# A decoder layer with product-key experts: 24 dense expert columns for 16, dense rows loaded ahead of the second product, and a finer-spread zero fill

## The chip, the cores and the metric

The kernel runs on one core of a Trainium2 chip. The metric is device microseconds (us) of one execution. Engines: PE is TensorE (matmuls; PEld its weight loads), DVE is VectorE, ACT is ScalarE, POOL is GpSimd and SP is SyncE, which here issues most of the DMAs. SPq rows are DMA issues of SP's queue.

## The reference, cut to what matters

One layer on 256 tokens of width 1024, all float32: a gated position mixer and an attention, their sum through `w_out`, a LayerNorm that gives `h`, the expert block below, and a last LayerNorm. The change touches the expert block alone, and the writing of zeros that prepares it:

```python
def peer_ffn(h, w_q, sub_keys, u_tab, v_tab):
    q = (xt @ w_q).reshape(n_tok, PEER_HEADS, 2, PEER_KEY_HALF)
    s = jnp.einsum('thpk,pnk->thpn', q, sub_keys)
    top_s, top_i = lax.top_k(s, PEER_TOPK)                    # 16 of 128 keys, twice
    ...                                                       # 16 of the 256 pairs: 16 of 128 x 128 experts
    gates = jax.nn.softmax(best_s, axis=-1)                   # for each of 8 heads
    hid = jax.nn.gelu(jnp.einsum('chkd,cd->chk', u_tab[ec], xc), approximate=False)
    y = jnp.einsum('chk,chkd->cd', gc * hid, v_tab[ec])
```

So each token picks 8 x 16 of 16,384 experts. An expert is a row of `u_tab` and a row of `v_tab`, both 1024 wide.

## The kernel before, in words

**Products.** Every float32 product is made of three matmuls on a split of each operand into `hi` and `lo` (fp32r). ACT writes `hi` (`do_hi`, line 125), DVE writes `lo` as the raw tile less `hi` (`do_lo`, line 135, its subtraction at line 145). Weight tiles of 128x1024 come through a ring of raw buffers: `do_load` (line 108) issues an SP load at line 121, or, for a tile whose rows stand in a list, an indirect DMA of POOL at line 117. `advance` (line 148) keeps three `hi` and two `lo` tiles ahead of PE and loads as far as raw buffers are free. The ring has 4 buffers, and from a point in U on 9 more (`RING`).

**The order.** All of the work is a list of steps, one weight tile each; the loop at line 1192 goes through it. At each step it advances the weight stream, calls the step's `before`, its matmuls, the previous step's `post` and the step's `after`, and then `run_stages`, which takes one turn of each generator in `stages`, and `run_queue`, which gives out some DVE work of the expert choice. What is written first stands first on each engine's queue.

**HG and its zeros.** `HG` is a DRAM array with a row for each expert: for both blocks of 128 tokens the hidden value and the gate. `fill_task` (line 274) writes zeros to its gates of block 0: the rows 0 and NX+1 to ROWS-1 whole (line 278, 127 rows in the second of the two), and then 32 fills of 256 KB (line 281), with three turns of the generator for each. It starts at step 16. `wo_before` (line 589), at the first step of the `w_out` product, runs all generators to their end, so all fills left are issued there.

**U.** The first expert product is dense: 128 tiles of 128 experts (`uexp_mm`, line 1042), all experts for all tokens. After every second tile ACT makes the GELU of both and SP writes them to HG (line 1056). The gates are added into HG by 128 indirect DMAs of POOL (line 752) for one block, and by a dense write for the other.

**V.** The second expert product takes `DENSE` = 16 tiles of 128 experts in a row, and 90 slot tiles whose 128 experts come from lists: two of `CAP_A` = 23 tiles of experts that tokens of one block alone use, and one of `CAP_B` = 44 for those of both blocks. The lists (`list_task`, line 973, its last line 1033) are made during U. A tile of a list costs POOL two gathers: rows of `peer_v` (line 117) and rows of HG (line 1098); a dense tile costs SP two loads (lines 121 and 1091). `wprep` (line 1101) multiplies hidden values and gates (DVE, line 1107) and splits the product into `wsp` (ACT line 167, DVE line 168); `vexp_mm` (line 1111, matmuls at line 1120) makes 12 matmuls of 512 columns for a tile of both blocks, 6 for one of one block. `slots` (line 1073) is the order: six dense tiles, then both, A, both, B and so on, with the other dense tiles put between. `vexp_before` (line 1160) loads HG rows `HG_AHEAD` = 6 tiles ahead and prepares `wsp` two ahead; at tile 0 it calls `v_open`. Experts beyond the lists' capacity would go through `overflow` (line 1127), behind a branch at line 1139.

**The end.** The last tiles' matmuls (line 1224) close the four sums, then come the residual, LayerNorm and the stores (lines 1226 to 1261).

Of the kernel before, what the change touches and what calls it, by code (L numbers as in the profile page):

```python
# [28 lines left out]
NK = 128  # L29
# [5 lines left out]

U_, V_, Q_, K_, VV_, GA_, GB_ = range(7)
NX = NK * NK
ROWS = NX + 128
ROW = 2 * T
CAP_A, CAP_B = 23, 44  # L40
SLOTS = 2 * CAP_A + CAP_B
DENSE, FIRST = 16, 6
UNITS = DENSE + SLOTS
COLG = 8
LISTG = 8
FILL = 4
HG_AHEAD = 6
RING = 9
RAW_BUFS = 4
HI_AHEAD = 3  # L50
LO_AHEAD = 2
# [8 lines left out]
def block_kernel(ctx, tc, a, out):  # L60
# [7 lines left out]
    def open_pool(name, **kw):  # L68
        kw.setdefault("bufs", 1)
        es = ExitStack()  # L70
        pool = es.enter_context(tc.tile_pool(name=name, reuse_waits="tile", **kw))
        return pool, es
# [9 lines left out]
    def acc(shape=(128, 512)):  # L82
        return ps1.tile(list(shape), F32, name="acc", tag="acc", bufs=4)
# [12 lines left out]
    ring, ring_pos, load_cap = [], [0], [None]  # L96

    def add_item(src, shape, dst=None, pieces=1):
        items.append((src, shape, dst, pieces))
        return len(items) - 1  # L100
# [65 lines left out]
    def split_to(hi, lo, src):  # L166
        nc.scalar.copy(hi, src)  # L167
        nc.vector.tensor_sub(lo, src, hi.bitcast(F32))  # L168
# [6 lines left out]
    def run_stages():  # L175
        for g in list(stages):
            try:
                next(g)
            except StopIteration:
                stages.remove(g)  # L180
# [13 lines left out]
    def drain_queue():  # L194
        while queue:
            try:
                if next(queue[0]) is None:
                    raise RuntimeError("background work waits for a later step")
            except StopIteration:
                queue.popleft()  # L200


    def mm3(ps, lh, ll, rh, rl, start, stop):
        for i, (l, r) in enumerate(((lh, rh), (lh, rl), (ll, rh))):
            nc.tensor.matmul(ps, l, r, start=start and i == 0, stop=stop and i == 2)  # L205
# [31 lines left out]
    def row_bcast(dst, src):  # L237
        n = src.shape[-1]
        nc.sync.dma_start(dst, bass.AP(tensor=src.tensor, offset=src.offset, ap=[[0, 128], [1, n]]))
# [16 lines left out]
    def step(item, mm, post=None, before=None, after=None, hi_cap=None, lo_cap=None):  # L256

        steps.append((item, mm, post, before, after, hi_cap, lo_cap))
# [11 lines left out]
    nc.vector.memset(zero, 0.0)  # L270
    HG = dram.tile([ROWS, 2, 2, 128], F32, name="HG")
    hview, *gview = dram_disjoint_views(HG[:, :, :, :], 2 + TOPK)

    def fill_task():

        for r in (slice(0, 1), slice(NX + 1, ROWS)):
            n = r.stop - r.start
            nc.sync.dma_start(HG[r, :, :, :].rearrange("r t w c -> r (t w) c"), zero[:n, None, :].to_broadcast([n, 4, 128]))
        rows = HG[1:NX + 1, :, :, :].rearrange("(p r) t w c -> p r t w c", p=128)
        for r in range(0, NK, FILL):  # L280
            nc.sync.dma_start(rows[:, r:r + FILL, 0, 1, :], zero[:, None, :].to_broadcast([128, FILL, 128]))
            yield
            yield
            yield
    eps = const.tile([128, 1], F32, name="eps")
# [604 lines left out]
    def gate_pass():  # L890
# [40 lines left out]
        def save():  # L931
# [6 lines left out]
            cell["vp"] = vp  # L938
            ring.extend([(vp, "raw2", RING)] * RING)
            ring_pos[0] = RAW_BUFS  # L940
# [101 lines left out]
    def uexp_mm(it, i):  # L1042
        wh, wl = parts.pop(it)
        if i % 2 == 0:
            hid[i // 2] = acc((128, 2, T))
        ps = hid[i // 2]
        for k in range(8):
            mm3(ps[:, i % 2, :], wh[:, k, :], wl[:, k, :], cell["hh"][:, k, :], cell["hl"][:, k, :], k == 0, k == 7)

    def uexp_post(i):  # L1050
        ps = hid.pop(i // 2)
        h = cell["keep"].tile([128, 2, T], F32, name="hid", tag="hid", bufs=2)
        nc.scalar.activation(h, ps, AF.Gelu)
        for k in range(2):
            r = (i - 1 + k) * NK + 1
            nc.sync.dma_start(hview[r:r + NK, :, 0, :], h[:, k, :].rearrange("p (t c) -> p t c", t=2))

    uit = [add_item(a["peer_uT"][i], [128, 8, 128]) for i in range(NK)]
    for i in range(NK):
        step(uit[i], lambda i=i: uexp_mm(uit[i], i), (lambda i=i: uexp_post(i)) if i % 2 else None)  # L1060

    def v_open():
        drain_queue()
        for n in range(HG_AHEAD):
            hg_load(n)
        cell["z"] = hpool.tile([128, 2, D], F32, name="z", tag="hh")
        cell["ln2"] = hpool.tile([128, 2, D], F32, name="ln2", tag="hl")
        nc.sync.dma_start(cell["z"], cell["res_d"])
        row_bcast(cell["ln2"][:, 0], a["ln2_g"])
        row_bcast(cell["ln2"][:, 1], a["ln2_b"])  # L1070
# [16 lines left out]
    def hg_load(n):  # L1087
        kind, s = slots[n]
        hg = cell["vp"].tile([128, 2, 2, 128], F32, name="hg", tag="hg", bufs=HG_AHEAD + 1)
        if kind == 3:  # L1090
            nc.sync.dma_start(hg, HG[1 + s * NK:1 + (s + 1) * NK, :, :, :])
            hgs[n] = hg
            return
        if kind == 2:
            dst, src = hg.rearrange("p t w c -> p (t w c)"), HG[:, :, :, :].rearrange("r t w c -> r (t w c)")
        else:
            dst, src = hg[:, 0].rearrange("p w c -> p (w c)"), HG[:, :, :, :].rearrange("r t w c -> (r t) (w c)")
        nc.gpsimd.indirect_dma_start(dst, None, src, bass.IndirectOffsetOnAxis(ap=cell["grow"][:, s:s + 1], axis=0))  # L1098
        hgs[n] = hg

    def wprep(n):

        m = len(TOKS[slots[n][0]])
        hg = hgs.pop(n)
        w = cell["vp"].tile([128, 2, 2, 128], F32R, name="wsp", tag="wsp", bufs=3)
        hv = hg[:, :m, 0, :]
        nc.vector.tensor_mul(hv, hv, hg[:, :m, 1, :])  # L1107
        split_to(w[:, 0, :m], w[:, 1, :m], hv)
        wsp[n] = w
# [50 lines left out]
    def vexp_before(n):  # L1160
        if n == UNITS - EARLY:
            overflow()
        if n == 8:
            cell["reg"] = nc.values_load(cell["extra"][0:1, 0:1], min_val=0, max_val=NX)
        if n == 0:
            while stages:
                run_stages()
            ps1_es.close()
            yp, cell["y_es"] = open_pool("yp", space=PSUM)
            ys = {k: yp.tile([128, 512], F32, name=f"y{k[0]}{k[1]}") for k in ((1, 0), (1, 1), (0, 0), (0, 1))}  # L1170
            cell["Y"] = [[ys[t, c] for c in range(2)] for t in range(2)]
            v_open()
            wprep(0)
            wprep(1)
        if n + HG_AHEAD < UNITS:
            hg_load(n + HG_AHEAD)
        if n + 2 < UNITS:
            wprep(n + 2)

    vit = []  # L1180
    for n, (kind, s) in enumerate(slots):
        if kind == 3:
            vit.append(add_item(a["peer_v"][s * NK:(s + 1) * NK, :].rearrange("p (a b) -> p a b", a=2), [128, 2, 512]))
        else:
            vit.append(add_item(a["peer_v"], [128, 2, 512]))
            row_lists[vit[n]] = lambda s=s: cell["vrow"][:, s:s + 1]
        step(vit[n], lambda n=n: vexp_mm(n), None, lambda n=n: vexp_before(n))
# [4 lines left out]
    for n, (item, mm, post, before, after, hi_cap, lo_cap) in enumerate(steps):  # L1192
        if pending and item == vit[0]:
            pending()
            pending = None
        advance(item, hi_cap, lo_cap)
        early_consts(n)
        if n == FILL_AT:
            stages.append(fill_task())
        if n == BIAS_AT:  # L1200
            stages.append(bias_task())
        if before:
            before()
        if n < len(steps) - EARLY:
            mm()
        if pending:
            pending()
        pending = post
        if after:
            after()  # L1210
        run_stages()
        run_queue(AUX_BUDGET)
# [121 lines left out]
```

## Time and profile before

| | us |
|---|---|
| median of 3 runs | 1081.35 (1080.59 to 1082.46) |
| the profiled execution | 1080.72 |
| its span | 1079.0 |
| U, dense product over 128 tiles, ends about | 776 |
| V begins | 785 |
| mean granted clock of TensorE, of full speed | 0.974 |

PE is busy 997.8 us of the span (92%), DVE 764.5 (71%), ACT 515.0 (48%) and POOL 449.2 (42%). These shares are averages over stages with different limits; the prediction reads single stages. A timeline row gives the start and the duration of one instruction (or of a run of like ones), and in brackets the idle time of its engine just before it and what ended that. A windows row gives a stretch and its length, the busy time and the instructions (x) of PE, PEld, DVE, ACT and POOL in it, PE's granted clock as a share of full speed, the mean busy share of the 16 DMA engines, and GB/s.

### The profile page before, as it was taken

To read this page: it belongs to the slowest core of one execution; us is meant where nothing else is said; L and a number is where in the kernel's file an instruction comes from. 1 tells how busy PE (TensorE), PEld (TensorE's weight loads), DVE (VectorE), ACT (ScalarE), POOL (GpSimd) and SP (SyncE) were. 2 spreads that over 40 slices of the span, in tenths; PEclk is the share of its full clock that TensorE was granted. 3 is DMA by queue.
4 is the path that set the end of the run, shared out by engine and by line. 5 is a ranking of instruction groups with operands and counts; after the bars stand their busy time and mean duration, and the time that the engine had idled before them with its cause. 6 is when DMAs were issued, how large, how long until landed. Compare 5 with 4: busy or idle time off the path is not lost. (4 is left out here: it accounts for less than half of the span.)

```text
span 1079.0 us, 18829 instructions
## 1 busy us (share of the span) xinstructions
PE 997.8 (92%) x7066; PEld 906.5 (84%) x7066; DVE 764.5 (71%) x1442; ACT 515.0 (48%) x747; POOL 449.2 (42%) x315
## 2 busy tenths in 40 slices
PE   9998999995999999989999999999789888998884
PEld 6988999994799999979999999999777666776663
DVE  6865655573779999997877769744367666666667
ACT  6535655542545554544355543344345444454443
POOL 0000000000000478778777873000257778787670
PEclk9999999997999999999999999999989999899998
DMA  7768556888455689887878889997888887878761
GB/s 274 273 205 281 160 181 205 275 270 252 142 215 170 165 223 217 217 208 187 185 186 193 179 227 325 306 387 227 245 285 273 281 285 258 272 263 270 247 195 44
DMA packets 151038, 249.60 MB, mean 231 GB/s; under 512 B 29360, under 2 KB 97881, under 8 KB 150553
## 3 DMA queue, kind: packets, MB, share of 16 engines
q1 hardware_dynamic: 113817, 183.47, 52.3%
q0 software_dynamic: 37120, 64.83, 23.9%
q8 instruction: 57, 0.93, 0.3%
q14 instruction: 44, 0.36, 0.1%
HBM read 212.26 MB, written 37.56 MB: 232 GB/s over the span
## 5 line engine op out<-in xcount | busy, mean ns | idle before, releaser
L145 DVE TENSOR_TENSOR lo<-raw,hi 128x1024 fp32r<-128x1024 f32 (+1 forms) x340 | 412.0, 1214 | 117.7 <-PE acc L205 63.7
L132 ACT CAST hi<-raw 128x1024 fp32r<-128x1024 f32 (+1 forms) x340 | 354.1, 1044 | 289.6 <-PE acc L205 157.4
L752 POOL DMA_INDIRECT HG<-gates,gidx x128 | 229.9, 1796 | 384.4 <-DVE ts L786 321.4
L205 PE MATMUL acc<-h_hi,hi 128*128 128x256 f32 x1152 | 327.8, 285 | 0.3 <-ACT hi L132 0.3
L205 PE MATMUL acc<-h_hi,lo 128*128 128x256 f32 x1152 | 324.9, 282 | 3.4 <-DVE lo L145 3.3
L205 PE MATMUL acc<-h_lo,hi 128*128 128x256 f32 x1152 | 322.2, 280 | 0.0
L1120 PE MATMUL y<-hi,wsp 128*128 128x512 f32 x664 | 223.7, 410 | 41.0 <-ACT wsp L167 34.7
L205 PEld LDWEIGHTS acc<-h_hi,lo 128*128 128x128 f32 x1152 | 217.1, 188 | 7.5 <-DVE lo L145 6.4
L205 PEld LDWEIGHTS acc<-h_hi,hi 128*128 128x128 f32 x1152 | 217.4, 189 | 0.6 <-ACT hi L132 0.5
L205 PEld LDWEIGHTS acc<-h_lo,hi 128*128 128x128 f32 x1152 | 217.5, 189 | 0.0
L1120 PEld LDWEIGHTS y<-hi,wsp 128*128 128x128 f32 x664 | 128.2, 193 | 87.0 <-ACT wsp L167 47.5
L117 POOL DMA_INDIRECT raw<-in_peer_v,vrow x90 | 103.2, 1147 | 146.2 <-DMA raw<-in_peer_v 95.3
L1120 PE MATMUL y<-lo,wsp 128*128 128x512 f32 x332 | 133.5, 402 | 0.0
L1098 POOL DMA_INDIRECT hg<-HG,grow x90 | 111.3, 1236 | 33.3 <-issue 23.8
L167 ACT CAST wsp<-hg 128x256 fp32r<-128x256 f32 (+1 forms) x106 | 38.1, 359 | 126.7 <-DVE hg L1107 82.4
L205 PE MATMUL acc<-xh,hi 128*128 128x256 f32 x320 | 92.9, 290 | 0.0
L205 PE MATMUL acc<-xh,lo 128*128 128x256 f32 x320 | 91.3, 285 | 0.0
L205 PE MATMUL acc<-xl,hi 128*128 128x256 f32 x320 | 91.2, 285 | 0.0
L1120 PEld LDWEIGHTS y<-lo,wsp 128*128 128x128 f32 x332 | 64.1, 193 | 13.5
L168 DVE TENSOR_TENSOR wsp<-hg,wsp 128x256 fp32r<-128x256 f32 (+1 forms) x106 | 39.0, 368 | 49.7 <-ACT wsp L167 37.8
L1107 DVE TENSOR_TENSOR hg<-hg 128x256 f32<-128x256 f32 (+1 forms) x106 | 38.5, 363 | 39.3 <-DMA hg<-HG,grow 28.9
L205 PEld LDWEIGHTS acc<-xl,hi 128*128 128x128 f32 x320 | 62.2, 194 | 0.2
(254 smaller groups left out, 1271.4 us busy)
## 6 DMA issues: line engine op xcount, KB each, us to landing
raw<-in_peer_uT SPq DMA_DIRECT2D x128, 512.0 KB
HG<-hid SPq DMA_DIRECT2D x128, 128.0 KB
HG<-zero SPq DMA_DIRECT2D x32, 256.0 KB
raw<-in_w_qk SPq DMA_DIRECT2D x16, 512.0 KB
raw<-in_w_q SPq DMA_DIRECT2D x16, 512.0 KB
HG<-G SPq DMA_DIRECT2D x16, 512.0 KB
raw<-in_peer_v SPq DMA_DIRECT2D x16, 512.0 KB
raw<-in_w_u SPq DMA_DIRECT2D x8, 512.0 KB
```

The lines of the kernel that those rows point to most:

```text
L117: nc.gpsimd.indirect_dma_start(r.rearrange("p a b -> p (a b)"), None, items[i][0], bass.IndirectOffsetOnAxis(ap=row_lists[i](), axis=0))
L132: nc.scalar.copy(parts[i][0][:, c], raws[i][:, c])
L145: nc.vector.tensor_sub(lo[:, c], r[:, c], hi[:, c].bitcast(F32))
L167: nc.scalar.copy(hi, src)
L168: nc.vector.tensor_sub(lo, src, hi.bitcast(F32))
L205: nc.tensor.matmul(ps, l, r, start=start and i == 0, stop=stop and i == 2)
L752: ins = nc.gpsimd.indirect_dma_start(gview[k].rearrange("r t w (c o) -> (r t w c) o", o=1), bass.IndirectOffsetOnAxis(ap=gidx[:, c:c + 1], ...
L1098: nc.gpsimd.indirect_dma_start(dst, None, src, bass.IndirectOffsetOnAxis(ap=cell["grow"][:, s:s + 1], axis=0))
L1107: nc.vector.tensor_mul(hv, hv, hg[:, :m, 1, :])
L1120: nc.tensor.matmul(cell["Y"][t][c], w[:, wp, j, :], v[q][:, c, :], start=(t, c) not in started, stop=n == last[t] and wp == 1)
```

## The change

There are 24 dense tiles instead of 16, and the lists shrink to 22, 22 and 40 tiles: 84 slot tiles for 90, 108 tiles in all for 106. A function `dense_start` is added, called after each U tile: at tile 120 of 128 it empties the queue of list work, runs the generators until the ring has its second part, and issues the HG loads of the first six dense tiles; at tile 127 it prepares `wsp` of tiles 0 and 1. `v_open` and `vexp_before` lose that work. HG rows are loaded 8 tiles ahead instead of 6, and the second part of the ring has 8 buffers for 9. The zero fill puts out a fill at every second step instead of every third, and ROWS is one larger, so that the fill at its end covers 128 rows.

```diff
--- before.py
+++ after.py
@@ -35,17 +35,17 @@
 
 U_, V_, Q_, K_, VV_, GA_, GB_ = range(7)
 NX = NK * NK
-ROWS = NX + 128
+ROWS = NX + 129
 ROW = 2 * T
-CAP_A, CAP_B = 23, 44
+CAP_A, CAP_B = 22, 40
 SLOTS = 2 * CAP_A + CAP_B
-DENSE, FIRST = 16, 6
+DENSE, FIRST = 24, 6
 UNITS = DENSE + SLOTS
 COLG = 8
 LISTG = 8
 FILL = 4
-HG_AHEAD = 6
-RING = 9
+HG_AHEAD = 8
+RING = 8
 RAW_BUFS = 4
 HI_AHEAD = 3
 LO_AHEAD = 2
@@ -279,7 +279,6 @@
         rows = HG[1:NX + 1, :, :, :].rearrange("(p r) t w c -> p r t w c", p=128)
         for r in range(0, NK, FILL):
             nc.sync.dma_start(rows[:, r:r + FILL, 0, 1, :], zero[:, None, :].to_broadcast([128, FILL, 128]))
-            yield
             yield
             yield
     eps = const.tile([128, 1], F32, name="eps")
@@ -1055,13 +1054,25 @@
             r = (i - 1 + k) * NK + 1
             nc.sync.dma_start(hview[r:r + NK, :, 0, :], h[:, k, :].rearrange("p (t c) -> p t c", t=2))
 
+    def dense_start(i):
+
+        if i == NK - 8:
+            drain_queue()
+            while len(ring) == RAW_BUFS:
+                run_stages()
+            for n in range(FIRST):
+                hg_load(n)
+        if i == NK - 1:
+            wprep(0)
+            wprep(1)
+
     uit = [add_item(a["peer_uT"][i], [128, 8, 128]) for i in range(NK)]
     for i in range(NK):
-        step(uit[i], lambda i=i: uexp_mm(uit[i], i), (lambda i=i: uexp_post(i)) if i % 2 else None)
+        step(uit[i], lambda i=i: uexp_mm(uit[i], i), (lambda i=i: uexp_post(i)) if i % 2 else None,
+             lambda i=i: dense_start(i))
 
     def v_open():
-        drain_queue()
-        for n in range(HG_AHEAD):
+        for n in range(FIRST, HG_AHEAD):
             hg_load(n)
         cell["z"] = hpool.tile([128, 2, D], F32, name="z", tag="hh")
         cell["ln2"] = hpool.tile([128, 2, D], F32, name="ln2", tag="hl")
@@ -1170,8 +1181,6 @@
             ys = {k: yp.tile([128, 512], F32, name=f"y{k[0]}{k[1]}") for k in ((1, 0), (1, 1), (0, 0), (0, 1))}
             cell["Y"] = [[ys[t, c] for c in range(2)] for t in range(2)]
             v_open()
-            wprep(0)
-            wprep(1)
         if n + HG_AHEAD < UNITS:
             hg_load(n + HG_AHEAD)
         if n + 2 < UNITS:
```

What this does to the order of instructions is shown at three places. First SP's queue at the start of the `w_out` product, before and then after; L281 is a zero fill.

```order
L121 DMA raw<-in_w_out 128x1024 x2
L281 DMA HG<-zero 128x4x128 x13
L239 DMA bc_l1g<-in_ln_g 128x1024
L239 DMA bc_l1b<-in_ln_b 128x1024
L239 DMA bc_pgb<-in_ple_b_gate 128x1024
L601 DMA iota<-in_iota 128x128
L602 DMA keysT<-in_keysT 128x256
L121 DMA raw<-in_w_out 128x1024
```

```order
L121 DMA raw<-in_w_out 128x1024 x2
L281 DMA HG<-zero 128x4x128 x4
L239 DMA bc_l1g<-in_ln_g 128x1024
L239 DMA bc_l1b<-in_ln_b 128x1024
L239 DMA bc_pgb<-in_ple_b_gate 128x1024
L600 DMA iota<-in_iota 128x128
L601 DMA keysT<-in_keysT 128x256
```

Thirteen fills in a row have become four; nine of them now stand earlier, among the weight loads of the products before. The next place is SP's queue at the end of U, before and after; L1056 (L1055 after) writes hidden values to HG, L1091 (L1102) loads rows of dense tiles from HG, and `raw` of `in_peer_v` are V's dense weight tiles.

```order
L121 DMA raw_9136<-in_peer_v 128x1024
L121 DMA raw_9166<-in_peer_v 128x1024
L1056 DMA HG<-hid 256x1x128 x12
L121 DMA raw_9495<-in_peer_v 128x1024
L1091 DMA hg<-HG 128x512 x6
L1068 DMA z<-res_d 128x2048
```

```order
L1055 DMA HG<-hid 256x1x128 x2
L121 DMA raw_9185<-in_peer_v 128x1024
L1102 DMA hg<-HG 128x512 x6
L1055 DMA HG<-hid 256x1x128 x6
L121 DMA raw<-in_peer_v 128x1024
L1055 DMA HG<-hid 256x1x128 x4
L1079 DMA z<-res_d 128x2048
```

The six HG loads moved from behind the last write of hidden values to ahead of the last ten writes. The third place is POOL at the same point; L752 (L751) is the last of the gate additions, L117 gathers rows of `peer_v`, L1098 (L1109) rows of HG.

```order
L752 DMA HG<-gates_3217,gidx 8454144x1 x128
L117 DMA raw_9201<-in_peer_v,vrow 128x1024
L117 DMA raw_9231<-in_peer_v,vrow 128x1024
L117 DMA raw_9266<-in_peer_v,vrow 128x1024
L117 DMA raw_9296<-in_peer_v,vrow 128x1024
L117 DMA raw_9331<-in_peer_v,vrow 128x1024
L117 DMA raw<-in_peer_v,vrow 128x1024 x4
L1098 DMA hg<-HG,grow 128x512
L117 DMA raw_9552<-in_peer_v,vrow 128x1024
L1098 DMA hg<-HG,grow 128x256
```

```order
L751 DMA HG<-gates_3217,gidx 8454656x1 x128
L117 DMA raw_9215<-in_peer_v,vrow 128x1024
L117 DMA raw_9262<-in_peer_v,vrow 128x1024
L117 DMA raw<-in_peer_v,vrow 128x1024 x3
L117 DMA raw_9422<-in_peer_v,vrow 128x1024
L117 DMA raw_9457<-in_peer_v,vrow 128x1024
L117 DMA raw_9499<-in_peer_v,vrow 128x1024
L1109 DMA hg<-HG,grow 128x512
L1109 DMA hg<-HG,grow 128x256
L1109 DMA hg<-HG,grow 128x512
L117 DMA raw_9540<-in_peer_v,vrow 128x1024
L1109 DMA hg<-HG,grow 128x256
```

Ahead of the first HG gather stand eight gathers of `peer_v` where nine stood, and three HG gathers now follow on one another before the next of `peer_v`.

## Rows read from the trace of the kernel before

**Rows 1.** Windows: stretch, length, PE PEld DVE ACT POOL, clock, DMA, GB/s; V, U.
```profile
791.00:1037.00 246.00, 217.71 (x882) 165.41 (x881) 166.75 (x275) 121.98 (x184) 193.50 (x161) 0.98 0.81 266
837.00:891.00 54.00, 45.11 (x185) 33.71 (x184) 35.43 (x59) 25.24 (x39) 43.01 (x37) 1.00 0.84 282
648.00:702.00 54.00, 52.75 (x485) 52.04 (x485) 46.10 (x76) 20.17 (x23) 7.73 (x5) 1.00 1.02 318
```

**Rows 2.** Timeline of POOL: start us, us, line, operation; start and middle of V.
```profile
781.99 0.96 POOL L1098 DMA_INDIRECT hg<-HG,grow  x1 [6.15 <-DMA raw<-in_peer_v]
791.21 0.95 POOL L117 DMA_INDIRECT raw<-in_peer_v,vrow  x1 [8.26 <-ACT hi L132]
...
846.08 1.76 POOL L117 DMA_INDIRECT raw<-in_peer_v,vrow  x1 [0.30 <-issue]
...
850.20 0.96 POOL L117 DMA_INDIRECT raw<-in_peer_v,vrow  x1 [0.30 <-ACT wsp L167]
```

**Rows 3.** Timeline of POOL near the end of V, its last row the last gather.
```profile
1037.04 0.96 POOL L1098 DMA_INDIRECT hg<-HG,grow  x1 [0.30 <-issue]
...
1049.19 1.74 POOL L1098 DMA_INDIRECT hg<-HG,grow  x1 [0.30 <-DVE wsp L168]
```

**Rows 4.** Timeline of SP's queue, DVE and PE between U and V.
```profile
779.02 2.96 SPq L1091 DMA_DIRECT2D hg<-HG  x6
...
784.17 0.42 DVE L1107 TENSOR_TENSOR hg<-hg 128x256 f32<-128x256 f32 x1 [6.73 <-DMA hg<-HG]
785.09 0.80 PE L1120 MATMUL y<-hi,wsp 128*128 128x512 f32 x1 [8.97 <-ACT wsp L167]
```

**Rows 5.** Timeline of SP's queue, ACT and PE at the start of the w_out product.
```profile
237.21 11.30 SPq L281 DMA_DIRECT2D HG<-zero  x13
...
253.02 0.69 SPq L121 DMA_DIRECT2D raw<-in_w_out  x1
...
261.42 1.04 ACT L132 CAST hi<-raw 128x1024 fp32r<-128x1024 f32 x1 [16.60 <-DMA raw<-in_w_out]
...
262.52 0.79 PE L205 MATMUL acc<-hi,mh 128*128 128x512 f32 x1 [10.68 <-ACT hi L132]
```

**Rows 6.** Timeline of SP's queue behind the fill of 127 rows.
```profile
56.50 11.15 SPq L281 DMA_DIRECT2D HG<-zero  x1
```

**Rows 7.** Windows, columns as in rows 1, of four stretches ahead of U.
```profile
63.00:66.00 3.00, 3.00 (x17) 2.56 (x16) 2.49 (x5) 1.36 (x2) 0.00 (x0) 1.00 0.07 22
90.00:95.00 5.00, 2.20 (x17) 1.94 (x16) 2.45 (x2) 3.88 (x6) 0.00 (x0) 1.00 0.98 353
108.00:162.00 54.00, 54.00 (x435) 53.31 (x435) 34.09 (x74) 31.78 (x70) 0.00 (x0) 1.00 0.55 171
263.00:269.00 6.00, 5.53 (x13) 4.13 (x13) 2.96 (x6) 2.69 (x5) 0.00 (x0) 0.50 0.37 124
```

**Rows 8.** Timeline of DVE, subtractions of lo alone, mid V and its end.
```profile
845.80 1.22 DVE L145 TENSOR_TENSOR lo<-raw,hi 128x1024 fp32r<-128x1024 f32 x1
...
850.25 1.22 DVE L145 TENSOR_TENSOR lo<-raw,hi 128x1024 fp32r<-128x1024 f32 x1
...
1046.84 1.22 DVE L145 TENSOR_TENSOR lo<-raw,hi 128x1024 fp32r<-128x1024 f32 x1
...
1048.88 1.22 DVE L145 TENSOR_TENSOR lo<-raw,hi 128x1024 fp32r<-128x1024 f32 x1
...
1051.29 1.22 DVE L145 TENSOR_TENSOR lo<-raw,hi 128x1024 fp32r<-128x1024 f32 x1
```

**Rows 9.** Timeline of PE in the middle of V.
```profile
848.07 0.39 PE L1120 MATMUL y<-lo,wsp 128*128 128x512 f32 x1
...
849.00 0.39 PE L1120 MATMUL y<-lo,wsp 128*128 128x512 f32 x1
```

**Rows 10.** Lines 168 and 1033: count, ns min/median/max, first and last start.
```profile
L168 DVE TENSOR_TENSOR wsp<-hg,wsp x106: 291/424/429, 785.1 to 1063.6; 128x256 fp32r<-128x256 f32 x60, 128x128 fp32r<-128x128 f32 x46
...
L1033 DVE CAST grow<-rows x1: 179/179/179, 688.1 to 688.1; 128x44 uint32<-128x44 f32 x1
```

## The prediction

> **What bounds the kernel now.** I read the views in this order: the windows table for the stage called V here (the second expert product, line 1120, from 785 us on), then the POOL timeline, then the seam between U (the first expert product) and V, then the two places before U where the zero fill stands.
>
> V first. Between 791 and 1037 us POOL is busy 193.50 us with 161 instructions [rows 1]; the idle piece ahead of each is 0.30 us [rows 2], so 193.5 + 161 x 0.30 = 241.8 of 246 us. POOL runs without a free moment; PE is busy 217.71 us, DVE 166.75, the DMA engines 0.81. The instructions are the two gathers of a slot tile (128 listed experts): its rows of peer_v and its rows of HG. From the start at 791.21 to the start at 1037.04 [rows 2, 3] the order has 161 steps: 245.83 / 161 = 1.527 us each. A dense tile (128 experts in a row) goes over SP and costs POOL nothing. So V is paced by the number of gathers, not by matmuls.
>
> Then the seam. PE stands for 8.97 us ahead of its first V matmul, at 785.09, waiting for a wsp tile; SP issues the six dense HG loads only at 779.02, behind the last writes of hid, and DVE uses their data at 784.17 [rows 4]. POOL's first HG gather, at 781.99, has waited for the last hid rows; the next peer_v gather starts at 791.21, since its buffer is freed by a subtraction that waits for PE [rows 2].
>
> Before U: at the start of the w_out product SP puts out 13 zero fills in 11.30 us, and the last w_out load stands behind them, at 253.02; PE waits 10.68 us, to 262.52 [rows 5], and then works at a granted clock of 0.50, which is the lower of its two levels, 1.2 GHz [rows 7]. Earlier, behind a fill of 127 rows, one issue takes 11.15 us [rows 6] while the DMA engines show a share of 0.07 and 22 GB/s [rows 7].
>
> **The change part by part.** The sum is made on the profiled execution: span 1079.0 us, 1080.72 with the 1.72 around it; the median is 1081.35.
>
> Gathers. The tiles go from 16 + 90 to 24 + 84, so gathers go from 180 to 168. Read in the built order: 8 stand ahead of the first HG gather (9 before), and from that gather to the one after which only HG gathers follow there are 154 steps. I start the new chain where the first HG gather stands today, 781.99: the last hid rows are issued where they were, and in the order three HG gathers follow on one another with free buffers, so the hole to 791.21 goes away.
>
> The price of a step. A gather takes 0.95 to 0.96 us when it is alone and up to 1.76: the one at 846.08 begins 0.28 us into the subtraction of 845.80 to 847.02 and ends 0.82 us after it; the one at 850.20 begins just ahead of a subtraction and takes 0.96 [rows 2, 8]. So 1.527 is 1.25 (0.95 and 0.30) and 0.277 of waiting for DVE. The subtractions per step go from 96 tiles on 161 steps to 101 on 154, a factor of 1.10: 0.277 becomes 0.305, the step 1.555. The chain is 154 x 1.555 = 239.5 us, and ends at 1021.5 (at 1.527: 235.2 and 1017.2). Bounds for the step, from the same rows: 1.48 if fewer starts meet a subtraction, 1.65 if more do; that is -11.6 and +14.6 us.
>
> The trace makes a gather wait for a subtraction of two SBUF tensors. The Trainium skill's page "SBUF — State Buffer", section "Who interferes with whom", infers that such a tensor_tensor does not hold up descriptor generation, though it contends with GpSimd's reads. By the first half of that the step would stay 1.527, 4.3 us less; I go by the rows.
>
> The end. After 1037.04 the kernel takes 41.96 us to the end, and POOL's last gather begins at 1049.19 [rows 3]: ten tiles are left, on DVE at 2.04 us for one with half its tokens and 2.41 for a full one (the distances of the last three subtractions in [rows 8]): six halves and four full, 21.9 us. After the change seven are left, five halves and two full: 15.0. So 41.96 becomes 35.1, and the span before the early gains 1021.5 + 35.1 = 1056.6.
>
> PE and DVE as cover. PE has 36 more matmuls (12 for a full tile, 6 for a half): 1,032 of 0.233 us (four starts in 0.93 us, [rows 9]) are 240.7 us, from about 777 to 1018. DVE: 64 x 2.41 + 44 x 2.04 = 244.0, to about 1021 and then 15.4 of the last tile's matmuls, LayerNorm and stores, as the last wsp product stands at 1063.6 now [rows 10]. Both end ahead of 1056.6, but by less than now: in the middle, where a dense tile comes every 4.4 slots, POOL needs 4.42 x 2 x 1.555 = 13.7 us, DVE 12.2, PE 12.1. The additional matmuls therefore cost nothing; without POOL's cover they are 8.4 us.
>
> Loads of dense rows moved into U. SP gets six loads of 256 KB at tile 120 of 128, ahead of hid writes; queued behind them are those writes and through them ACT's GELU, which has two hid buffers, each for two tiles. The six take 2.96 us to issue [rows 4]. I cost this at nothing; the uncovered price is 3 us. Two products for the first tiles (wprep) move ahead of PE's last U tile on DVE and ACT: 1.7 us, beside the last tile's 24 matmuls, nothing. drain_queue has nothing left to drain, the last of the lists being done at 688.1 us [rows 10]. Eight raw buffers for nine, and nine hg for seven: counted in the order above.
>
> Zero fill. At the w_out product 4 fills are left for 13. 9 x 0.87 (11.30 / 13, [rows 5]) = 7.8 us earlier for the last w_out load; PE's wait goes from 10.7 to about 2.9. Next late is that load's own landing, 8.4 us from issue to the cast. Upper bound 10.7 and the low clock's price, which is 13 matmuls [rows 7] at twice the 0.233 of [rows 9], 3.0 more: 13.7. Lower bound 5. The nine fills go into 57 to 237 us, where PE waits little and the DMA engines have room, 0.55 from 108 to 162 us with PE busy throughout [rows 7]: cost 1, bounds 0 to 4. The 128-row fill: 22 GB/s is what one of sixteen engines would carry, so 508 pieces went down one; 512 can be spread. The waits that follow at 90 to 95 us leave PE 2.20 of 5 us busy [rows 7]: I take 2 of these 2.8, bounds 0 to 4. Together -8.8.
>
> Sum: 1056.6 - 8.8 = 1047.8 of span, 1049.5 for the execution, 0.63 more on the median: **1050**.
>
> **The rivals.** (a) The DMA engines pace V. The tiles' bytes rise from 77.3 to 79.2 MB (64 full tiles of 786 KB, 44 halves of 655 KB). Without the 14 peer_v and 6 HG tiles already in SBUF, but with z and the LayerNorm rows, 72.4 MB remain; at the 266 GB/s of [rows 1] 272 us from 782, and 28 us from the last landing to the end (1051 to 1079): 1082 - 8.8 + 1.7 = 1075. For it: the share is 0.81. Against: 0.84 and 282 GB/s in 837 to 891, and 1.02 and 318 GB/s in U [rows 1], so there is room. The Trainium skill's page "DMA: Bandwidth & Descriptors", section "Issuing engines are not separate DMA queues", says that DMAs of SP and POOL share the same 16 engines: by that rule the move from POOL to SP saves issue time alone. The trace agrees, but issue time is what V lacks.
>
> (b) Slower than before: POOL's gathers wait for DVE much more often. Were each to start inside a subtraction, like the one of 846.08, a step is 2.06 us, the time 1127. From a step of 1.76 on all that is gained is given back. For it: the denser DVE. Against: that would be 0.51 of waiting where 0.277 is measured, with 10 per cent more subtractions.
>
> (c) POOL no longer binds, since dense tiles let it run ahead: PE or DVE end at 1018 to 1021, the time is about 1030. Against: 13.7 us against 12.2.
>
> (d) The change doesn't do what it says: the early dense loads wait for the newest HG write, the seam's 9 us stay and the fifth gather waits for the first V tile, near 789.6: 3 to 6 us more, 1053 to 1056, within the forecast's range. Lists too short would be another thing: with the reference's inputs the 104 listed columns hold 2,651 and 2,684 experts of one half (2,816 places) and 4,960 of both (5,120), so the overflow branch stays unused; one too many would cost hundreds of us.
>
> **How the numbers follow.** Forecast, POOL-paced V with fewer gathers, 1032 to 1069: 0.76, (d) included. (a) 0.12; (c) 0.05; (b) 0.05; gains that cancel, 0.02. Its ends add the unknowns: the step at its low bound and the w_out gain at its upper one give 1050 - 11.6 - 5.9 = 1032; the step at its high bound, the w_out gain at 5 and the first fill's 2 us gone give 1050 + 14.6 + 2.8 + 2 = 1069. The range takes in (c) as well, 1030 to 1069, and leaves out 0.19: (a), (b) and the gains that cancel. A measurement of this kernel tells 0.2% from no change. Faster 0.93 (forecast, (a), (c)), same 0.02, slower 0.05.
>
> **What would show it.** In the profile after: POOL back to back from about 773 us on, given the early gain, with 154 steps of 1.5 to 1.6 us; a PE gap at the seam under 2 us; four fills and a PE wait of 2 to 5 us at the w_out product; no long issue behind the 128-row fill. I am wrong if POOL shows waits for buffers or data in V, if the step is above 1.65, if DMA share stands at 1.0 there, or if the earlier fills starve PE before 237 us.

## The result

The changed kernel takes 1051.21 us (median of 4 runs, 1049.66 to 1051.9) against 1080.97 of the kernel before in the same comparison: a ratio of 0.9733, 95% interval 0.9694 to 0.9773. Its profiled execution takes 1051.57 us, with a span of 1049.8 and a mean granted clock of 0.987. It was run once more beside later kernels:

> The changed kernel itself once more, beside the three others of this call: 1050 us within 3, on the chip on which they run.

1053.94 us (1050.05 to 1054.61) against 1085.02 of the kernel before on that chip, the ratio 0.9736 (0.9684 to 0.9788): both times are 0.3 to 0.4% longer there, the ratio is the same. The prediction was 1050 us, and 1047.8 for the span.

Where the time went shows in the places at which products begin and end. First lines of before and then of after, from the view of one source line: count, ns min/median/max, first and last start. `mh` stands in the w_out product, `h_hi` with `hi` first in the gate product behind it.

```profile
L205 PE MATMUL acc<-hi,mh x32: 389/389/793, 235.3 to 271.1; 128*128 128x512 f32 x32
L205 PE MATMUL acc<-hi,h_hi x32: 392/396/397, 279.1 to 301.1; 128*128 128x512 f32 x32
...
L205 PE MATMUL acc<-h_hi,lo x1152: 274/278/415, 302.1 to 775.8; 128*128 128x256 f32 x192
...
L1120 PE MATMUL y<-hi,wsp x664: 390/398/796, 785.1 to 1065.6; 128*128 128x512 f32 x166
```

```profile
L205 PE MATMUL acc<-hi,mh x32: 387/389/628, 231.1 to 259.1; 128*128 128x512 f32 x32
L205 PE MATMUL acc<-hi,h_hi x32: 392/396/397, 267.0 to 289.0; 128*128 128x512 f32 x32
...
L205 PE MATMUL acc<-h_hi,lo x1152: 273/280/416, 290.0 to 762.0; 128*128 128x256 f32 x192
...
L1131 PE MATMUL y<-hi,wsp x688: 387/389/632, 762.1 to 1034.6; 128*128 128x512 f32 x172
```

The last column has the same marks in the second profile of the changed kernel, the one taken beside later kernels.

| us from the span's start | before | after | difference | after, second profile |
|---|---|---|---|---|
| first matmul of the w_out product | 235.3 | 231.1 | -4.2 | 233.0 |
| first matmul of the gate product behind it | 279.1 | 267.0 | -12.1 | 268.9 |
| last matmul of U | 775.8 | 762.0 | -13.8 | 763.4 |
| first matmul of V | 785.1 | 762.1 | -23.0 | 763.5 |
| last matmul of V | 1065.6 | 1034.6 | -31.0 | 1033.0 |
| end of the span | 1079.0 | 1049.8 | -29.2 | 1048.3 |

So there are three gains: 14 us up to the end of U (1 of them, a difference between executions, already stands at the 30th us, ahead of any fill), 9 us at the seam between U and V, and 8 us in V. Behind V 2 us are lost again. Two profiles of the same kernel differ by up to 2 us at these marks and by 2.9 in V (272.4 and 269.5 us), so a smaller difference between two single profiles can be chance.

### The profile page after: what moved, and what is told of

Read it like the earlier page. It is cut to its first block, busy times and chain, and to the rows that moved or that the text cites. A ratio compares the mean times of both kernels' runs of the same rounds, so it can differ in the third digit from the quotient of the medians.

```text
span 1049.8 us, 18905 instructions
## 1 busy us (share of the span) xinstructions
PE 993.2 (95%) x7094; PEld 905.3 (86%) x7094; DVE 764.5 (73%) x1444; ACT 516.8 (49%) x751; POOL 445.6 (42%) x303
## 5 line engine op out<-in xcount | busy, mean ns | idle before, releaser
L751 POOL DMA_INDIRECT HG<-gates,gidx x128 | 228.9, 1788 | 372.2 <-DVE ts L785 308.4
L1131 PEld LDWEIGHTS y<-hi,wsp 128*128 128x128 f32 x688 | 130.5, 190 | 67.7 <-ACT wsp L167 40.2
L117 POOL DMA_INDIRECT raw<-in_peer_v,vrow x84 | 107.8, 1284 | 137.0 <-DMA hg<-HG 100.5
L1131 PE MATMUL y<-lo,wsp 128*128 128x512 f32 x344 | 135.8, 395 | 0.0
L1109 POOL DMA_INDIRECT hg<-HG,grow x84 | 104.6, 1245 | 28.2 <-issue 18.6
L205 PEld LDWEIGHTS acc<-xh,hi 128*128 128x128 f32 x320 | 61.4, 192 | 0.2
```

Of the source, the lines that this page charges most:

```text
L117: nc.gpsimd.indirect_dma_start(r.rearrange("p a b -> p (a b)"), None, items[i][0], bass.IndirectOffsetOnAxis(ap=row_lists[i](), axis=0))
L751: ins = nc.gpsimd.indirect_dma_start(gview[k].rearrange("r t w (c o) -> (r t w c) o", o=1), bass.IndirectOffsetOnAxis(ap=gidx[:, c:c + 1], ...
L1131: nc.tensor.matmul(cell["Y"][t][c], w[:, wp, j, :], v[q][:, c, :], start=(t, c) not in started, stop=n == last[t] and wp == 1)
```

## The profile after

At the w_out product (answers to [rows 5]; timeline of SP's queue, ACT and PE):

```profile
233.16 2.96 SPq L281 DMA_DIRECT2D HG<-zero  x4
...
241.56 0.38 SPq L121 DMA_DIRECT2D raw<-in_w_out  x1
...
249.16 1.04 ACT L132 CAST hi<-raw 128x1024 fp32r<-128x1024 f32 x1 [8.56 <-DMA raw<-in_w_out]
```

```profile
250.25 0.50 PE L205 MATMUL acc<-hi,mh 128*128 128x512 f32 x1 [2.63 <-ACT hi L132]
```

Four fills stand where 13 stood, and PE waits 2.63 us instead of 10.68. Behind the fill of 128 rows (answers to [rows 6] and to the second row of [rows 7]; timeline of SP's queue, then a window):

```profile
54.08 1.35 SPq L278 DMA_DIRECT2D HG<-zero  x2
55.47 0.62 SPq L281 DMA_DIRECT2D HG<-zero  x1
```

```profile
90.00:95.00 5.00, 5.00 (x43) 4.95 (x42) 1.21 (x3) 3.97 (x5) 0.00 (x0) 1.00 1.03 372
```

The issue of 11.15 us is now 0.62, and PE is busy in all of the 5 us of which it had 2.20.

At the seam (answers to [rows 2, 4]; SP's queue, PE, and then POOL):

```profile
739.09 3.17 SPq L1102 DMA_DIRECT2D hg<-HG  x6
```

```profile
762.03 0.28 PE L205 MATMUL acc<-h_hi,lo 128*128 128x256 f32 x1
762.14 0.40 PE L1131 MATMUL y<-hi,wsp 128*128 128x512 f32 x1
```

```profile
769.05 1.00 POOL L1109 DMA_INDIRECT hg<-HG,grow  x1 [2.92 <-DMA HG<-hid]
770.35 0.97 POOL L1109 DMA_INDIRECT hg<-HG,grow  x1 [0.30 <-issue]
771.62 1.16 POOL L1109 DMA_INDIRECT hg<-HG,grow  x1 [0.30 <-DVE lo L145]
773.09 1.79 POOL L117 DMA_INDIRECT raw<-in_peer_v,vrow  x1 [0.30 <-issue]
...
1011.58 1.18 POOL L1109 DMA_INDIRECT hg<-HG,grow  x1 [0.30 <-DMA raw<-in_peer_v,vrow]
...
1020.52 1.73 POOL L1109 DMA_INDIRECT hg<-HG,grow  x1 [0.30 <-DVE wsp L168]
```

The first V matmul follows the last of U without a gap, and POOL goes from its first HG gather on without the hole of 8.26 us. From 769.05 to 1011.58 there are 154 steps, 1.575 us each. The window of V (answers to the first row of [rows 1], the same columns):

```profile
770.00:1010.00 240.00, 219.47 (x915) 169.60 (x913) 170.48 (x282) 124.27 (x190) 193.69 (x153) 0.99 0.84 289
```

193.69 + 153 x 0.30 = 239.6 of 240 us: POOL is still never free. A gather's mean is 1.266 us (193.69 / 153) where it was 1.202 (193.50 / 161). In the second profile the same steps lie between 770.59 and 1010.47 us and take 1.558 each.

## The experiments

Three kernels make one part of the change each, from the kernel before. Each comparison is with runs of the kernel before on the same chip.

**The fill alone.**

```diff
-ROWS = NX + 128
+ROWS = NX + 129
...
-            yield
             yield
             yield
```

> The kernel before with the changed zero fill alone (a fill every second step, last block of 128 rows). Theory: all work behind the w_out product moves ahead by what its stalls lose: 7.9 us at w_out and about 3 us in the first 135 us, as in the trace of the changed kernel, so about 1081 - 11 = 1070 us. Rival: the stretch up to U is hidden behind GpSimd's gate additions in U, which end as late as before, and the time stays within 2 us of 1081.

1073.12 us against 1082.16, ratio 0.9891 (0.9841 to 0.9942): 9 us less by the medians, where 11 were expected; the interval, 6.3 to 17.2, holds both. The rival (hidden behind the gate additions of U) falls. Of the two edits, the one row more was also run alone:

> The kernel before with one row of HG more alone, so that the fill behind it covers 128 rows instead of 127. Theory (the fill of 127 rows goes through one DMA engine and holds up the weight loads behind it): no issue of 11 us behind it, and 2 to 3 us less: 1078 to 1079 us. Rival (the loads run far enough ahead of TensorE): 1081 within 1 us.

Ratio 0.9947 (0.9915 to 0.9978), 1078.8 us against 1085.15: 6 us less by the medians. The issue behind it takes 0.62 us there too. The interval, 2.4 to 9.2 us, holds the 3 us that the marks of the changed kernel's first profile give.

**The early loads alone.**

```diff
-HG_AHEAD = 6
-RING = 9
+HG_AHEAD = 8
+RING = 8
...
+    def dense_start(i):
...
-        for n in range(HG_AHEAD):
+        for n in range(FIRST, HG_AHEAD):
...
-            wprep(0)
-            wprep(1)
```

> The kernel before with the early HG loads and wsp tiles alone (dense_start, 8 tiles ahead, ring part of 8); 16 dense tiles and the old fill. Theory: GpSimd's chain of gathers runs on without the hole of 8.3 us ahead of the gather at 791.21, so V ends some 8 us earlier: 1073 us. Rival: the gap of 9 us is TensorE's alone, GpSimd's pace decides and takes it back: within 2 us of 1081.

1069.23 us, ratio 0.9871 (0.9813 to 0.9929): 12.9 us less, more than the 8 expected, though the interval, 7.7 to 20.2, holds them. In its profile V begins at 776.3 instead of 785.1 and lasts 279.3 us instead of 280.5. The rival (POOL's pace takes the seam back) falls.

**The dense tiles alone.**

```diff
-CAP_A, CAP_B = 23, 44
+CAP_A, CAP_B = 22, 40
...
-DENSE, FIRST = 16, 6
+DENSE, FIRST = 24, 6
```

> The kernel before with 24 dense tiles and lists of 22, 22 and 40 alone. Theory (V paced by GpSimd's gathers): 12 gathers fewer at 1.53 to 1.58 us are 18 us, less about 3 us by which the denser DVE work lengthens the other steps: 1066 us, 1063 to 1069. Rival (the DMA engines pace V): 1.9 MB more at 266 GB/s, 7 us slower, 1088. Rival (TensorE or DVE pace V): 8.4 or 7 us slower, 1088 to 1090.

1071.8 us, ratio 0.988 (0.9831 to 0.9929): 10.4 us less. That is short of the 15 expected and outside the 1063 to 1069 forecast, though the interval, 7.7 to 18.3, holds both; all rivals forecast a slower kernel. Its profile shows a part of what is missing: without the early loads POOL still stands at the seam, for 3.93 and then 8.33 us (timeline of POOL):

```profile
788.55 0.96 POOL L1098 DMA_INDIRECT hg<-HG,grow  x1 [3.93 <-DVE wsp L168]
797.84 0.95 POOL L117 DMA_INDIRECT raw<-in_peer_v,vrow  x1 [8.33 <-DMA raw<-in_peer_v]
```

The three parts together make 3.5%, with some 0.9 either way, against 2.7% for the change as a whole. Within that the runs don't tell whether the parts help or hinder each other.

**What paces V.** The next kernels start from the changed one. The most direct test takes half of POOL's gathers away; SP loads as many rows in their place, in order and not by the list:

```diff
+            nc.sync.dma_start(hg, HG[1 + s * NK:1 + (s + 1) * NK, :, :, :])
...
-        nc.gpsimd.indirect_dma_start(dst, None, src, bass.IndirectOffsetOnAxis(ap=cell["grow"][:, s:s + 1], axis=0))
```

> The changed kernel, with the HG rows of a listed tile loaded by SP as 128 rows in order instead of gathered by GpSimd by the list; what is added up for listed experts is therefore not the reference's. Bytes, products and matmuls are the same; GpSimd keeps 84 gathers of 168. Theory (GpSimd's gathers pace V, DVE's chain of 244 us and TensorE's 241 stand right behind): V falls from 272.5 us to about 250, 1026 to 1034 us in all. Rival (DVE's chain, TensorE or the DMA engines pace V as much): V stays above 265 us, 1044 us or more.

1027.13 us against 1053.94 of the changed kernel on the same chip. V takes 246.1 us (766.8 to 1012.9). Its window:

```profile
770.00:980.00 210.00, 208.73 (x898) 165.95 (x897) 165.18 (x276) 121.73 (x184) 72.63 (x75) 1.00 0.94 332
```

With POOL busy for a third of the time PE is busy nearly throughout, and the DMA engines move 332 GB/s where they moved 289. So POOL's gathers did hold V, and neither the DMA engines nor DVE's chain would have held it at 272 us. (Rows in order may cost the DMA engines less than rows by a list; but with lists too they move 315 and 321 GB/s in the kernels with 32 dense tiles below.)

**What stands behind POOL.** DVE makes a product, waits for ACT's cast of it and subtracts (0.41 to 0.52 us of waiting for each tile). The next edit makes the product one tile earlier:

```diff
+    def wmul(n):
+        m = len(TOKS[slots[n][0]])
+        hv = hgs[n][:, :m, 0, :]
+        nc.vector.tensor_mul(hv, hv, hgs[n][:, :m, 1, :])
...
+        if n + 3 < UNITS:
+            wmul(n + 3)
         if n + 2 < UNITS:
             wprep(n + 2)
```

> The changed kernel with the product of hidden values and gates made one tile earlier, so that DVE need not wait for ScalarE's cast between product and split (0.41 to 0.52 us for each of 108 tiles); gathers and subtractions are as before. Theory (GpSimd's gathers alone pace V, DVE only waits for them): V as long as now, at most 3 us less in the last seven tiles, 1047 to 1052 us. Rival (DVE's chain with ScalarE, 244 us of the 270 of V, paces V together with GpSimd): its 51 us of waiting go and V shortens by 10 us or more, under 1042 us.

1048.48 us, ratio 0.967 (0.962 to 0.9721) against 0.9733 and 0.9736 of the changed kernel. The intervals overlap; a gain of 3 to 7 us is likely but not shown. POOL's step is 1.554 us, as in the changed kernel's second profile (1.558). The rival, with 10 us or more, falls. Who waited for whom on DVE (in 760 to 1066 us; us in total, times, longest), in the changed kernel and then in this one, shows why:

```profile
DVE wsp L168 <- ACT wsp L167: 51.0, 108, 0.5
DVE hg L1118 <- DMA hg<-HG,grow: 25.4, 21, 2.2
```

```profile
DVE hg L1117 <- DMA hg<-HG,grow: 65.2, 36, 5.0
DVE wsp L168 <- ACT wsp L167: 2.6, 5, 1.4
```

The 51 us of waiting for ACT went, and DVE now stands 40 us longer for POOL's gathers: while POOL paces V, most of DVE's waiting costs nothing. With POOL out of the way it costs more:

> The kernel with HG rows of listed tiles by SP (the same part is changed), and with the product of hidden values and gates one tile earlier, which takes up to 51 us out of DVE's chain. Theory (with GpSimd and DVE out of the way TensorE's 241 us are the bound): V 245 us, 1020 to 1026 us. Rival (something else holds TensorE up as soon as it is the bound, as in the run with both edits, where DVE and ScalarE stood for 5 us at a time with no work of GpSimd or DVE ahead of them): V 255 us or more, 1032 us or more.

1013.73 us, 13.4 less than with POOL relieved alone, on the same chip. V takes 235.2 us:

```profile
770.00:980.00 210.00, 210.00 (x928) 173.87 (x927) 172.56 (x287) 125.93 (x192) 111.20 (x76) 1.00 0.95 345
```

This is TensorE's own time: 1,032 matmuls in 235.2 us are 0.228 each. It came out below the 1020 to 1026 expected, which had taken 0.233 from [rows 9] and some waits. The order of the bounds of V is thus read off: POOL 270 to 272 us, DVE's chain with its waits for ACT 246, TensorE 235.

**More dense tiles.**

```diff
-CAP_A, CAP_B = 22, 40
+CAP_A, CAP_B = 20, 38
...
-DENSE, FIRST = 24, 6
+DENSE, FIRST = 32, 6
```

> The changed kernel with 32 dense tiles and lists of 20, 20 and 38 tiles: 156 gathers, 110 tiles. Theory (GpSimd paces V): 12 steps of 1.58 us fewer, less what DVE's 250 us then hold back: 1034 to 1042 us. Rival (the DMA engines pace V): 2 MB more at 289 GB/s, 7 us slower, 1057. Rival (DVE's chain or TensorE paces V): 6 to 11 us slower, 1056 to 1062.

1043.15 us (1040.67 to 1043.56), ratio 0.961 (0.9559 to 0.966): faster, as POOL's pace has it, a microsecond above the range given. V takes 259.5 us. The rivals that make the bytes or the matmuls the bound gave 1056 or more. Then both edits together:

> 32 dense tiles (lists of 20, 20 and 38) and the product one tile earlier, all subtractions whole. Theory (with 12 gathers fewer GpSimd needs 142 steps of 1.6 us, 227 us, so that DVE's chain of 250 us had become the bound with 32 dense tiles; the earlier product takes 51 us out of it and TensorE's 252 us are next): 3 to 8 us less than with 32 dense tiles alone, 1034 to 1040 us. Rival (GpSimd still paces V with 32 dense tiles): within 2 us of that run, 1041 to 1045 us.

1035.81 us (1034.6 to 1038.94), ratio 0.9573 (0.9519 to 0.9627), within the range. Against 32 dense tiles alone the intervals overlap; in the two profiles V is 5.4 us shorter (254.1 for 259.5). It is faster than both kernels of this case. Its window has POOL at 179.35 + 144 x 0.30 = 222.6 of 225 us, still the bound, with PE close behind. The window of 32 dense tiles alone, shown first, has POOL as full (180.58 + 139 x 0.30 = 222.3), so the time came out as the theory has it, but that DVE's chain had taken POOL's place there isn't shown; POOL's step went from 1.594 to 1.550 us:

```profile
770.00:995.00 225.00, 221.50 (x952) 176.69 (x951) 172.58 (x287) 127.35 (x192) 180.58 (x139) 1.00 0.90 315
```

```profile
770.00:995.00 225.00, 221.72 (x955) 177.89 (x954) 167.79 (x287) 130.34 (x193) 179.35 (x144) 1.00 0.92 321
```

**The price of a step.** The prediction put the part of a step above 1.25 us down to DVE's long subtraction, inside which a gather stands. If so, two short subtractions hold it up less:

```diff
-        for c in cuts(i):
+        for c in (slice(0, 1), slice(1, 2)) if i in v_items else cuts(i):
             nc.vector.tensor_sub(lo[:, c], r[:, c], hi[:, c].bitcast(F32))
```

> The changed kernel with each lo subtraction of V as two instructions of 512 columns instead of one of 1024. Theory (a gather that starts inside a subtraction stands until that instruction ends, and this is what lengthens the step from 1.25 to 1.575 us): the longest gather falls from 1.76 to about 1.35 us, the step to about 1.42, 154 steps are 24 us shorter, and then TensorE or DVE end last, near 1018 plus 15 us: 1028 to 1036 us. Rival (the gathers are slowed by DVE's or the DMA engines' traffic as such, not by the length of one instruction): the step stays at 1.55 or more, DVE has 108 instructions more: 1050 to 1057 us.

Half of the theory holds and half fell. Lines of POOL's peer_v gathers, of the changed kernel and then of this one (ns min/median/max), and the window of this one:

```profile
L117 POOL DMA_INDIRECT raw<-in_peer_v,vrow x84: 944/1150/1951, 742.1 to 1010.3; - x84
```

```profile
L118 POOL DMA_INDIRECT raw<-in_peer_v,vrow x84: 946/958/1277, 743.4 to 1004.7; - x84
```

```profile
770.00:1010.00 240.00, 222.11 (x917) 170.59 (x917) 177.48 (x378) 125.93 (x189) 162.81 (x158) 0.99 0.87 296
```

The median gather falls from 1.150 to 0.958 us and the longest from 1.951 to 1.277; POOL's busy time falls by 31 us. But the time is 1054.08 us, ratio 0.9728 (0.968 to 0.9776), no gain, and V lasts 273.7 us. The time lies in the rival's range, but not for its reason: the gathers did get shorter. POOL now has idle time, 1 to 5.6 us at a time, and waits for buffers. DVE's chain, 7 us longer by the 108 instructions more, doesn't explain it, since a chain of 244 us let V pass in 246. So the split subtractions were run with the earlier product:

> The changed kernel with that earlier product and with each lo subtraction of V in two instructions. Theory (split subtractions do free GpSimd, and in the run with them alone DVE's longer chain took its place: 252 us and 16 us of waits): GpSimd at 1.33 us a step needs 205 us, DVE some 200, and TensorE with 1,032 matmuls, 241 us from 762, becomes the bound: 1003 plus 15 to 20 of the end and some waits, 1022 to 1032 us. Rival (landings of weight tiles pace V, as in the waits of 4.3 us in that run): 1045 us or more.

1053.89 us, ratio 0.9746 (0.9678 to 0.9814): again no gain, and the theory that DVE's chain was what replaced POOL falls. The time is in the range of the rival (late weight tiles); the waits speak for something else. What waited for what in this run (in 765 to 1040 us; engine, line, waited for: us in total, times, longest):

```profile
ACT hi L133 <- PE y L1136: 81.2, 49, 4.3
ACT hi L133 <- remote: 34.9, 6, 8.3
...
DVE lo L146 <- remote: 23.6, 5, 6.7
```

and one place of its timeline:

```profile
802.79 0.96 POOL L1112 DMA_INDIRECT hg<-HG,grow  x1 [0.30 <-issue]
805.71 1.29 DVE L146 TENSOR_TENSOR lo<-raw,hi 128x512 fp32r<-128x512 f32 x2 [5.32 <-remote]
805.75 1.04 ACT L133 CAST hi<-raw 128x1024 fp32r<-128x1024 f32 x1 [5.82 <-remote]
...
807.16 0.50 PE L1136 MATMUL y<-hi,wsp 128*128 128x512 f32 x1 [4.16 <-ACT wsp L168]
```

DVE and ACT stand together for over 5 us and go on together; both then use tiles that PE frees, though PE's records show its matmuls of those tiles as over. "remote" means that the profile has no instruction for what released them. The semaphore records of this trace tell more: what both wait for is PE's semaphore, not a landing. It has no update between 798.55 and 805.68 us, though four matmuls that give one end at 799.12 to 802.99; then seven updates stand within 0.33 us, while PE is idle. So PE's signals came late and in a bunch. Two updates of PE closer together than 0.15 us occur 50 and 49 times in V in the two kernels with split subtractions, and at most 10 times in any other trace of this case. ACT's waits without a known releaser are 2 us with the earlier product alone (2 of them, the longest 1.3 us). What delays PE's signals when the subtraction is split wasn't settled.

## Why the prediction was right

**The total** was right to 1.2 us of the median, partly by luck: terms that were off by 3 to 4 us nearly cancelled. POOL's chain was put at 781.99 - 8.8 = 773.2 for its start and measured at 769.05 (-4.1); its 154 steps at 1.555 and measured at 1.575 (+3.1); the end at 35.1 us and measured at 1049.84 - 1011.58 = 38.3 (+3.2). Together +2.1: 1047.8 became 1049.8. In the second profile the same terms are off by -2.6, +0.4 and +2.7, together +0.5. So an early start and a late end are there in both, and the step was right to within what two executions differ by.

**Gathers set V: right.** The count of 154 was exact, POOL has no free moment, and the run with half of its gathers takes V down to 246 us. As covers the working took 240.7 for PE and 244.0 for DVE and saw correctly that both end earlier; the runs put them at 235 and 246.

**The price of a step: right in cause, at most 0.02 us low.** For denser subtractions the working raised the waiting from 0.277 to 0.305; measured are 1.575 - 1.25 = 0.325, and 0.308 in the second profile. The split shows the cause directly: with the subtraction cut in two, for the same bytes and the same elements, the longest gather of `peer_v` fell from 1.951 to 1.277 us. The Trainium skill's page "SBUF — State Buffer", section "Who interferes with whom", infers that a tensor_tensor of two SBUF operands doesn't hold up descriptor generation, and says that it contends with GpSimd's reads of SBUF. Here such an instruction does hold up a gather; a gather also reads its list of rows from SBUF, and whether this read or the descriptor generation stands, no run shows.

**Zero fill: the w_out term right, the first fill right or a little small.** Predicted 7.8, measured 7.9 (12.1 - 4.2), and 7.9 again in the second profile; PE's wait was put at 2.9 and is 2.63 (3.35 in the second). The fill of 128 rows was taken at 2 us and gives 3.2 (4.2 less the 1.0 of the first 30 us): the waits of 90 to 95 us went altogether. In the second profile 0.9 us of them are left and the fill gives 2.2. The crowding of 1 us isn't there; PE is busy in all of 100 to 200 us, as before. Of the 4.1 us by which the chain starts early these terms make 2.3; 1.0 stands in the first 30 us and 0.8 in U, where no step of the prediction put anything, and these are no more than two executions differ by.

**The seam: right.** The loads don't wait for the newest HG write (rival (d)), SP's six issues cost U nothing, and the gap fell from 8.97 us to none. Run alone, this part has in its profile 8.8 us at the start of V, 1.2 in V and 1.5 behind it.

**The end: 3.2 us too short.** 1.9 us of it stand between DVE's last instruction and the end of the span (timelines of DVE, before and after):

```profile
1074.15 1.42 DVE L1260 SCALAR_TENSOR_TENSOR z<-z,l2rs,ln 128x512 f32<-128x512 f32 x2
```

```profile
1043.13 1.42 DVE L1269 SCALAR_TENSOR_TENSOR z<-z,l2rs,ln 128x512 f32<-128x512 f32 x2
```

From their ends it is 3.4 us before (to 1079.0) and 5.3 after (to 1049.84). The last store is done 2.1 us behind DVE in both. What differs is POOL's closing DRAIN, which every engine waits for (view of the last line, before and after; its longest is the one meant, and it is also the first):

```profile
L1329 POOLq DRAIN  x3: 46/157/6294, 1070.4 to 1078.7; - x3
```

```profile
L1338 POOLq DRAIN  x3: 46/113/9641, 1039.3 to 1049.6; - x3
```

It ends at 1076.7 before, ahead of the last store, and at 1049.0 after, 2.4 us behind it. It goes with the kernel: the time behind DVE's last instruction is 5.3 us in all six traces with 168 gathers, 4.3 in both with 156, and 3.3 to 3.5 in those with 180 or 84. No term of the prediction has it, and why it is longer no run shows. Of the other 1.3 us a wait of DVE for an HG gather takes 0.84:

```profile
1016.88 0.42 DVE L1118 TENSOR_TENSOR hg<-hg 128x256 f32<-128x256 f32 x1 [0.84 <-DMA hg<-HG,grow]
```

**The rivals.** (a), V paced by the DMA engines, is excluded: 32 dense tiles moved more bytes in less time, and 345 GB/s were reached in V. The Trainium skill's page "DMA: Bandwidth & Descriptors", section "Issuing engines are not separate DMA queues", says that DMAs of all issuing engines run on the same 16 DMA engines, and that issuing from several saves issue time alone. This case agrees: with 84 gathers moved from POOL to SP the bytes stayed, and the issue time that POOL lost made V 246.1 us long instead of 269.5 to 272.4. (b) would have needed a step of 1.76 and the step is 1.575. (c) didn't happen, since POOL is never free in V; with 32 dense tiles it comes close, with PE busy for 221.50 of 225 us.

## What to carry to other kernels

When an engine's timeline shows the same short gap ahead of every instruction, count its instructions and multiply: when that fills the stretch, as 239.6 of 240 us here, the engine may be the bound although its busy share is 81%. An instruction moved to another queue is worth at most its step: 12 gathers fewer, some 18 us by their steps, gave 10 us when done alone, and the next 12 gave 8 to 14. Then take that engine out in an experiment and read the next bounds off, before spending work on them: here 272, 246 and 235 us stood in a row, and the edit worth some 3 to 7 us at first, not clear of noise, was worth 13 once the first bound was out of the way. A part of a stall that is explained by one instruction can be shortened without the time following, so measure the time and not the stall.

## What the runs showed of the hardware

An indirect DMA of GpSimd that is issued while DVE runs a subtraction of two float32 SBUF tiles ends about 0.8 us after it, wherever it began. In the changed kernel's V 85 gathers begin inside one and end 0.81 to 1.17 us after it, 0.83 in the median. In that trace a gather takes 0.95 us alone and up to 1.95 beside subtractions of 1.22 us; with two of half the length one behind the other, and nothing else changed, it takes up to 1.28 (rows of `peer_v`) or 1.43 (rows of HG). So a gather gets through between two DVE instructions that follow without a pause; it doesn't need DVE to be idle.

Behind a fill of 127 rows the next issue took 11.15 us, while the DMA engines moved 22 GB/s; behind one of 128 rows it took 0.62 us.
